# Where the transfers of weight sums are queued, and which engine spreads the probabilities

## The chip, the cores and the metric

The kernel runs on one core of a Trainium2 chip. The metric is device time in microseconds from one launch to its end; lower is better. The core has a matrix engine (TensorE, PE in the profile, with its weight loads as PEld), VectorE (DVE), ScalarE (ACT), GpSimd (POOL) and SyncE (SP). SP and POOL issue most of the DMA transfers.

## What is computed

One layer of a hybrid decoder trunk on 256 positions of 2048 channels, in float32. The input is normalised and projected at once into the inputs of three branches and their gates:

```
h = RMSNorm_pre(x); p = h @ w_in
A: GLU -> causal depthwise conv (31) -> LayerNorm -> swish -> @ w_a_out
B: gelu(uv); u * (tril(W_s) LN(v) + b) per 128-position chunk -> @ w_b_out
C: sparse attention: shared queries, separate K/V for compressed / selected / window -> @ w_c_out
y = (g_A*A + g_B*B + g_C*C) @ w_o ;  x = x + RMSNorm_post(y)
h = RMSNorm_pre(x); u = causal_dwconv3(h @ w_up); x = x + RMSNorm_post((silu(u_g) * u_v) @ w_down)
```

The compressed keys and values of branch C come from blocks of 32 positions: `hid = silu(blocks @ w1)`, then `hid @ w2`. The probabilities over the compressed blocks multiply the compressed values, and the other two branches of the attention are added.

## The kernel before, in words

**Products.** Each float32 weight tile of 128x1024 is fetched by SP into one of five buffers (`fetch`, L117), rounded by ScalarE into a high part (L199) and subtracted by VectorE into a low part (L200). TensorE multiplies high by high, high by low and low by high; the two parts of the activations stay in SBUF. Four buffers of each part lie between the splits and TensorE. In the later stages the same is done at L1011 and the products at L1055.

**Products saved.** For part of the gate columns, the output projection and the down projection, four blocks of a product over pairs of 128x512 weight blocks are made with seven products instead of eight (`Seven`). These need sums and differences of weight blocks. The sums are made long before by DMA alone: `ahead_steps` lists, for each quadruple of blocks, a copy into a buffer in DRAM, a second copy where three or four sums are wanted, and transfers that add onto what has been copied. `ahead_by(mark, n)` has POOL wait until a marked value is there (the copy into `tick`, L159, shown at the line of the helper, L129) and then issue the next `n` transfers of the list. `pooled` holds all of these in one order on POOL; a transfer that adds waits on POOL for the copy it adds to. There are 204 transfers in the list: 64 for the gates, 16 for the output projection, 124 for the down projection.

**Order of the stages.** First the second half of branch B's input, then branch A's input (16 transfers behind it, two for each of eight steps), the first half of branch B's input (16 more), the compression's input, the keys, the values, the queries (16, two for each of eight steps, L796). Then `branch`: for four quarters of 512 columns, merge gates and the outputs of branch B (4, 8, 8 and 8 transfers behind a quarter, L1204). Then `outs_a`, the second branch's outputs in the title of the change: the outputs of branch A in four quarters (8 behind each, L1226). Then the merge gates by `Seven` (`gates_7`), the outputs of branch C, the output projection, the up projection, the down projection. What is left of the list is spread over 42 of the 44 steps of the up projection (L1638).

**Background work.** Work that isn't a plain product lies in a queue of generators, `bg`: branch B's normalisation, branch A's convolution and normalisation, the compression (`cmp_prep`, `cmp_gen`), the attention (`attn`). `pump(ns)` is called between plain products and runs generators until the sum of the nanoseconds that they yield reaches the budget (6500 a call in `branch` and `outs_a`); what is yielded is a booking, not a wait. Once the attention has begun (the mark "attn"), the budget of a call is multiplied by `RUSH`, 0.85. The order on each engine follows from this order of emission and a scheduler's estimate of when each instruction could start; at run time each engine keeps that order.

**Compression.** `cmp_prep` has POOL clear the last column of a buffer (L687), then VectorE and ScalarE form the two parts of the blocks (`bk`). `cmp_gen` fetches `w1` in four pieces and multiplies into `zp` (L709, L711), booking 2300 ns for each piece. It starts once the second quarter of the merge gates is at its third part (the mark "outputs").

**Attention.** Eight units (two halves of the positions, two groups of heads, selected and window) each make scores, weights and values. For every second unit, four in all, the transposed probabilities over the compressed blocks are spread over four heads by one multiplication of 128x512 elements (L990), on POOL, into `spread`, a part of the buffer `vbd`. TensorE reads it at L922 as the first product into the unit's output `O`.

Of the kernel before, what the change touches and what calls it, by code (L numbers as in the profile page):

```python
# [45 lines left out]

GP, GREST = [0, 1, 2, 3], list(range(8, KT))
OP, OREST = [0, 1, 2, 4], [6, 7, *range(10, KT)]
BA, BB, BC, BG, RUSH, SUMS_AT = 2100, 2200, 2200, 6500, 0.85, 4
PR = 1000  # L50
NW0, _ = 34, 6
S1, S2, S3 = 6, 12, 14
# [12 lines left out]
def block(ctx: ExitStack, tc: tile.TileContext, x, xf, x0, fp, cst, rows, sgw, w1, w2, wf_a, wt_bv, wf_bu, wf_c,  # L65
# [604 lines left out]
    spread = vbd[:, 2:6]  # L670
# [30 lines left out]
    def cmp_gen(kv):  # L701
        bk = bk_box[kv]
        zp = bank([128, 2, 256], f"zp{kv}")
        for q in range(4):
            hi, lo = piece(w1[kv, :, q * 1024:q * 1024 + 1024], 1024)
            for i in range(4):
                jj = 4 * q + i
                st = bk[:, jj].rearrange("p a n -> p (a n)")
                PE.matmul(zp[:, 0], lhsT=st, rhs=hi[:, i * 256:i * 256 + 256], start=(jj == 0), stop=(jj == 15),  # L709
                          skip_group_check=True)  # L710
                PE.matmul(zp[:, 1], lhsT=st, rhs=lo[:, i * 256:i * 256 + 256], start=False, stop=(jj == 15),  # L711
                          skip_group_check=True)
            yield 2300
        zs = [q1(f"zs{kv}{a}") for a in range(2)]
        for a in range(2):
            S.activation(zs[a], zp[:, a], AF.Copy)
        hp = bank([128, 2, 64], f"hp{kv}")
        for h in range(2):
            for a in range(2):
                PE.matmul(hp[:, h], lhsT=zs[a][:, h * 128:h * 128 + 128], rhs=sel, start=(a == 0), stop=(a == 1))  # L720
        w2s = q1(f"w2s{kv}", (128, 2, 128))
        nc.sync.dma_start(w2s, w2[:, kv])
        hid = P1.tile([128, 2, 64], F32, tag="hid", bufs=2, name=f"hid{kv}")
        th = q1(f"hth{kv}", (128, 2, 64))
        S.activation(th, hp, AF.Tanh, scale=0.5)
        hidden.append(V.scalar_tensor_tensor(hid, th, 1.0, hp, op0=ALU.add, op1=ALU.mult).ins)
        yield 400
        if kv == 0:
            ps = bank([128, 64], "kcp")
            for h in range(2):  # L730
                PE.matmul(ps, lhsT=w2s[:, h], rhs=hid[:, h],
                          start=(h == 0), stop=(h == 1))
            V.tensor_mul(kcb.rearrange("p g n -> p (g n)"), ps, cs[:, K_KM:K_KM + 64])
            yield 200
        else:
            hr = [q1(f"hidr{h}", (128, 2, 128)) for h in range(2)]
            for h in range(2):
                for gg in range(2):
                    V.tensor_copy(hr[h][:, gg].rearrange("p (j m) -> p j m", j=4),
                                  hid[:, h, gg * 32:gg * 32 + 32][:, None, :].to_broadcast([128, 4, 32]))  # L740
            yield 800
            for gg in range(2):
                ps = bank([128, 128], f"vcp{gg}")
                for h in range(2):
                    PE.matmul(ps, lhsT=hr[h][:, gg], rhs=w2s[:, h], start=(h == 0), stop=(h == 1))
                V.tensor_mul(vbd[:, gg], ps, cs[:, K_BM:K_BM + 128])
                yield 270
# [17 lines left out]
    for i in range(4):  # L765
        pc = ftile(wf_c[4 + i], hT)
        fsum(pc, kk[:, i % 2, i // 2], rb=rb)
        pump(BUDGET)
    vsw = kkv[:, 1].rearrange("p (t c) -> p t c", t=2)
    gsg = P1.tile([128, 2, 48], F32, name="gsg")  # L770
# [22 lines left out]
    for i in range(8):  # L793
        pq = ftile(wf_q[i], hT)
        fsum(pq, qf[:, i], scale=0.125, rb=rb)
        ahead_by(qf[:, i, 0:1], 2)  # L796
        pump(BUDGET)


# [43 lines left out]
    pct = {}  # L843
# [133 lines left out]
    def attn():  # L977

        units = [Unit(qt, gg, br) for qt in (1, 0) for gg in range(2) for br in range(2)]
        yield from in_turn(lnz_gen(), apart(cmp_attn(1)), apart(units[0].scores()))  # L980
        marks.add("A")
        Ct_box["t"] = s16(P1, [128, 8, 2, T], R, "Ct")
        for n, u in enumerate(units):
            if n + 1 < len(units):
                if n == 1:
                    yield from in_turn(apart(cmp_attn(0)), units[n + 1].scores())
                else:
                    yield from units[n + 1].scores()
            if u.at[2] == 0:
                G.tensor_mul(spread, pct[u.at[0]][:, u.at[1]][:, None, :].to_broadcast([128, 4, 128]),  # L990
                             cs[:, K_RJ:K_RJ + 4][:, :, None].to_broadcast([128, 4, 128]))
            yield from u.weights()
            if SUMS_AT <= n < SUMS_AT + 4:
                yield from input_sums(n - SUMS_AT)
            if u.at[2] == 0:
                O = bank([128, 4, 128], "O" + u.nm)
            yield from u.values(O)
# [149 lines left out]
    def branch():  # L1147

        for cb in range(4):
            pg = [PS.tile([128, 512], F32, tag="acc", name=f"pg0{cb}{t}") for t in range(2)]  # L1150
            for q in range(4):
                hs = granule(wt_g[cb * 4 + q])
                for k in range(4 * q, 4 * q + 4):
                    hi, lo = hs[(k % 4) // 2]
                    c = slice((k % 2) * 512, (k % 2) * 512 + 512)
                    for t in range(2):
                        ts = slice(t * 128, t * 128 + 128)
                        with ExitStack() as order:
                            if (cb, k) == (1, 0):
                                order.enter_context(tc.issue_after(norm["v"]))  # L1160
                            mm_t(pg[t], hT[:, k, 0, ts], hT[:, k, 1, ts], hi[:, c], lo[:, c], k == 0, k == KT - 1)
                if (cb, q) == (0, 2):
                    until("m")
                    debt[0] = 0.0
                elif q < 3:
                    if (cb, q) == (1, 2):
                        marks.add("outputs")
                    pump(BUDGET)
            tgs = {}
            for t in range(2):  # L1170
                for a in range(2):
                    tgs[t, a] = q1(f"mg0{cb}{t}{a}")
                    with tc.high_priority(offset=int(PR)):
                        gated[0] = S.activation(tgs[t, a], pg[t][:, a * 256:a * 256 + 256], AF.Tanh,
                                                scale=rh[:, t:t + 1]).ins
            marks.add("gates")
            pump(BUDGET)
            py = [PS.tile([128, 512], F32, tag="acc", name=f"py0{cb}{t}") for t in range(2)]
            for q in range(2):
                hs = granule(wt_p[cb * 2 + q])  # L1180
                if cb == 0 and q == 0:
                    until("B")
                act = Bt_box["t"]
                for k in range(4 * q, 4 * q + 4):
                    hi, lo = hs[(k % 4) // 2]
                    c = slice((k % 2) * 512, (k % 2) * 512 + 512)
                    for t in range(2):
                        ts = slice(t * 128, t * 128 + 128)
                        with ExitStack() as order:
                            if (cb, k) == (0, 7):  # L1190
                                until("v")
                                debt[0] = max(debt[0], 0.0)
                                order.enter_context(tc.issue_after(norm["v"]))
                            pe_last[0] = mm_t(py[t], act[:, k, 0, ts], act[:, k, 1, ts], hi[:, c], lo[:, c], k == 0, k == 7)
                if q == 0:
                    pump(BUDGET)
            for t in range(2):
                for a in range(2):
                    cc = slice(cb * 512 + a * 256, cb * 512 + a * 256 + 256)
                    y = mac[:, t, cc]  # L1200
                    with tc.high_priority(offset=int(PR)):
                        V.scalar_tensor_tensor(y, tgs[t, a], 1.0, py[t][:, a * 256:a * 256 + 256], op0=ALU.add,
                                               op1=ALU.mult)
            ahead_by(mac[:, 0, cb * 512:cb * 512 + 1], (4, 8, 8, 8)[cb])  # L1204
            pump(BUDGET)

    def outs_a():

        for cb in range(4):
# [13 lines left out]
            for t in range(2):  # L1223
                with tc.high_priority(offset=int(PR)):
                    V.tensor_copy(ya[:, t, cb * 512:cb * 512 + 512], py[t])
            ahead_by(ya[:, 0, cb * 512:cb * 512 + 1], (8, 8, 8, 8)[cb])  # L1226
            pump(BUDGET)

    def m_sums(n):
# [511 lines left out]
    i = 0  # L1741
# [260 lines left out]
```

## Time and profile before

| | us |
|---|---|
| three timed runs | 1578.43, 1580.05, 1580.97 |
| their median | 1580.05 |
| the profiled execution | 1574.79 |
| its span, first to last instruction | 1573.1 |
| mean granted clock of TensorE | 0.995 |

The profiled execution is one run of the program, recorded instruction by instruction. Busy times are for each engine; the waits of an engine name the instruction that ended the wait; the chain of waits follows the last instruction back to what released it; a granted clock of 0.50 means that TensorE ran at half speed in that stretch.

### The profile page before, as it was taken

The page shows a single profiled execution, that of the slowest core. Times are in us where ns is not written, and L with a number is a line of the kernel's source. Part 1 is how long each engine was busy: PE and PEld are TensorE (multiplying, and loading weights), DVE is VectorE, ACT ScalarE, POOL GpSimd, SP SyncE. Part 2 cuts the span into 40 slices and gives each one's busy share as a digit, 9 for nine tenths or more (in the row PEclk, how much of TensorE's full clock was granted, in tenths as well). Part 3 has the DMA queues.
Part 4 walks back from the last instruction along what each step waited for, and adds up shares of the span by engine and source line. Part 5 has one row for each costly group of instructions (what it writes and reads, how often), then busy time and mean ns, then how long its engine had stood idle before and what let it go on. Part 6 is the DMA issues. An engine that isn't in the chain of part 4 may idle for free.

```text
span 1573.1 us, 23354 instructions
## 1 busy us (share of the span) xinstructions
PE 1555.0 (99%) x8101; PEld 1317.6 (84%) x8101; DVE 1320.8 (84%) x2229; ACT 969.3 (62%) x1536; POOL 219.7 (14%) x351
## 2 busy tenths in 40 slices
PE   9999999999999898999999999999999999999998
PEld 8888889888777576888888888888888888888887
DVE  7899999787675477977986898888888887899898
ACT  7645454456767665656665766565656665677774
POOL 1011340211112220000000022222121212100000
PEclk9999999999999999999999999999999999999999
DMA  9687997998779997767774699999999999989895
GB/s 369 198 267 235 284 274 217 297 276 280 202 211 274 256 292 260 257 235 250 269 250 175 219 290 321 309 293 288 273 273 274 265 270 290 310 286 349 311 372 217
DMA packets 130712, 426.13 MB, mean 271 GB/s; under 512 B 15009, under 2 KB 16785, under 8 KB 129825
## 3 DMA queue, kind: packets, MB, share of 16 engines
q1 hardware_dynamic: 99648, 329.46, 59.7%
q0 software_dynamic: 30368, 94.52, 25.5%
q8 instruction: 63, 1.03, 0.3%
q10 hardware_dynamic: 576, 0.66, 0.1%
q14 instruction: 57, 0.46, 0.1%
HBM read 416.45 MB, written 90.44 MB: 322 GB/s over the span
## 4 chain that ended last, share of the span: by engine, by line
PE 90%; DMA 6%; DVE 2%; issue 1%; ACT 1%; POOL 1%; SPq 0%; DVEq 0%; ACTq 0%; POOLq 0%
PE ps L228 29%; PE ps L235 15%; PE pg L1055 7%; PE pd1a L1055 4%; PE pd0b L1055 4%; PE pd0a L1055 3%; PE pd1b L1055 3%; DMA ahead<-in_wt_dq_dram 2%; DMA ahead<-in_wt_oq_dram 2%; PE poa L1055 2%; PE py L250 2%; PE py L251 2%; PE py L249 2%; PE pg L250 1%; PE pg L251 1%; PE pg L249 1%
## 5 line engine op out<-in xcount | busy, mean ns | idle before, releaser
L200 DVE TENSOR_TENSOR wlo<-wraw,whi 128x1024 fp32r<-128x1024 f32 (+1 forms) x344 | 417.5, 1218 | 91.7 <-ACT whi L199 73.3
L199 ACT ACTIVATE whi<-wraw 128x1024 fp32r<-128x1024 f32 (+1 forms) x344 | 361.7, 1056 | 206.3 <-PE ps L228 117.2
L228 PE MATMUL ps<-h2T,whi 128*128 128x512 f32 x1360 | 317.2, 390 | 0.0
L228 PEld LDWEIGHTS ps<-h2T,whi 128*128 128x128 f32 x1360 | 252.4, 188 | 50.4
L235 PEld LDWEIGHTS ps<-h2T,wlo 128*128 128x128 f32 x1360 | 169.4, 192 | 3.6
L235 PE MATMUL ps<-h2T,wlo 128*128 128x256 f32 x1360 | 170.7, 283 | 0.0
L228 PE MATMUL ps<-hT,whi 128*128 128x512 f32 x640 | 151.9, 390 | 0.0
L228 PEld LDWEIGHTS ps<-hT,whi 128*128 128x128 f32 x640 | 117.9, 188 | 23.0
L1011 DVE TENSOR_TENSOR wlowraw<-wraw,whiwraw 128x1024 fp32r<-128x1024 f32 x74 | 89.8, 1222 | 42.8 <-ACT whiwraw L1011 40.8
L1011 ACT ACTIVATE whiwraw<-wraw 128x1024 fp32r<-128x1024 f32 x74 | 78.0, 1059 | 55.2 <-PE pg L1055 13.2
L556 DVE SCALAR_TENSOR_TENSOR cv<-hb,fps,cv 128x256 f32<-128x256 f32 x240 | 104.6, 478 | 0.1
L1055 PE MATMUL pg<-whiwraw,hT 128*128 128x512 f32 x256 | 85.3, 407 | 1.2 <-ACT whiwraw L1011 1.2
L1613 ACT ACTIVATE fa<-fs,fps 128x256 f32<-128x256 f32 x88 | 52.7, 599 | 53.5 <-DVE fs L274 51.7
L235 PEld LDWEIGHTS ps<-hT,wlo 128*128 128x128 f32 x640 | 81.1, 191 | 2.5
L235 PE MATMUL ps<-hT,wlo 128*128 128x256 f32 x640 | 82.8, 283 | 0.0
L129 POOL DMA_DIRECT2D ahead<-in_wt_dq_dram x91 | 69.4, 895 | 74.7 <-DMA ahead<-in_wt_dq_dram 72.1
L271 ACT ACTIVATE t<-ps 128x256 f32<-128x256 f32 x125 | 47.5, 381 | 49.5 <-PE ps L235 27.0
L129 POOL DMA_DIRECT2D ahead<-ahead x53 | 43.8, 827 | 206.9 <-DMA ahead<-in_wt_dq_dram 74.7
L129 POOL COPY tick<-gh 128x1 f32<-128x1 f32 x44 | 34.3, 781 | 236.1 <-ACT gh L1621 236.1
L1055 PEld LDWEIGHTS pg<-whiwraw,hT 128*128 128x128 f32 x256 | 49.6, 194 | 14.4 <-issue 2.1
L1614 DVE SCALAR_TENSOR_TENSOR fa<-fs,fps,fa 128x255 f32<-128x255 f32 x88 | 42.3, 481 | 16.6 <-ACT fa L1613 16.5
L1055 PE MATMUL pg<-wlowraw,hT 128*128 128x512 f32 x128 | 51.8, 404 | 3.3 <-DVE wlowraw L1011 3.3
(2519 smaller groups left out, 3313.7 us busy)
## 6 DMA issues: line engine op xcount, KB each, us to landing
wraw<-in_wf_up_dram SPq DMA_DIRECT2D x176, 512.0 KB, 6.4
ahead<-in_wt_dq_dram POOLq DMA_DIRECT2D x74, 512.0 KB, 9.4
wraw<-in_wt_p_dram SPq DMA_DIRECT2D x48, 512.0 KB, 5.9
wraw<-in_wt_dq_dram SPq DMA_DIRECT2D x33, 512.0 KB, 5.6
wraw<-in_wf_a_dram SPq DMA_DIRECT2D x32, 512.0 KB, 5.0
ahead<-in_wt_gq_dram POOLq DMA_DIRECT2D x32, 512.0 KB, 9.6
wraw<-in_wt_g_dram SPq DMA_DIRECT2D x32, 512.0 KB, 6.4
wraw<-in_wt_gp_dram SPq DMA_DIRECT2D x32, 512.0 KB, 5.4
```

The costliest lines, as they stand in the source:

```text
L129: in_pool[:] = [op(*args, **kw).ins]
L199: S.activation(hi[:, :n], raw[:, :n], AF.Copy)
L200: V.tensor_sub(lo[:, :n], raw[:, :n], hi[:, :n].bitcast(F32))
L228: ins = PE.matmul(ps, lhsT=ws[k // 8][0][:, c:c + 128], rhs=mov[:, k], start=bool(k == 0 and first), stop=bool(k == n - 1 and not first), ...
L235: ins = PE.matmul(ps[:, 1], lhsT=ws[k // 8][1][:, c:c + 128], rhs=mov[:, k, 0], start=bool(k == 0 and not first), stop=bool(k == n - 1 and ...
L249: PE.matmul(ps, lhsT=xh, rhs=hi, start=first, stop=False)
L250: PE.matmul(ps, lhsT=xh, rhs=lo, start=False, stop=False)
L271: S.activation(t1, ps[:, 1], AF.Copy)
L556: V.scalar_tensor_tensor(ca[:, j], hb[:, j, k:k + T], w(j, k), ca[:, j], op0=ALU.mult, op1=ALU.add)
L1011: seq[eng] = [op(*args, **kw).ins]
L1055: ins = PE.matmul(bank, lhsT=a[x], rhs=w[y], start=first and j == 0, stop=bool(last and j == 2), skip_group_check=more).ins
L1613: S.activation(a, s, AF.Identity, bias=fps[:, C_FB + f:C_FB + f + 1], scale=w[2])
```

## The change

The list of transfers and its order stay as they are; what changes is behind which step they are issued. One goes behind each of the four key projections (four in all), 20 instead of 16 behind the queries (two and three in turn), 8 instead of 4 behind the first quarter of `branch`, and 12 instead of 32 behind `outs_a` (8 and 4, none behind its last two quarters). Before the up projection 100 transfers are issued instead of 108, and the up projection gets the other 104. The multiplication that spreads the probabilities goes from POOL to VectorE. A piece of the compression is booked at 3200 instead of 2300 ns. `RUSH` goes from 0.85 to 1.0, so that a call of `pump` runs as much background work during the attention as before it.

```diff
-BA, BB, BC, BG, RUSH, SUMS_AT = 2100, 2200, 2200, 6500, 0.85, 4
+BA, BB, BC, BG, RUSH, SUMS_AT = 2100, 2200, 2200, 6500, 1.0, 4
...
                 PE.matmul(zp[:, 1], lhsT=st, rhs=lo[:, i * 256:i * 256 + 256], start=False, stop=(jj == 15),
                           skip_group_check=True)
-            yield 2300
+            yield 3200
...
         pc = ftile(wf_c[4 + i], hT)
         fsum(pc, kk[:, i % 2, i // 2], rb=rb)
+        ahead_by(kk[:, i % 2, i // 2, 0:1], 1)
         pump(BUDGET)
...
         fsum(pq, qf[:, i], scale=0.125, rb=rb)
-        ahead_by(qf[:, i, 0:1], 2)
+        ahead_by(qf[:, i, 0:1], 2 + i % 2)
         pump(BUDGET)
...
             if u.at[2] == 0:
-                G.tensor_mul(spread, pct[u.at[0]][:, u.at[1]][:, None, :].to_broadcast([128, 4, 128]),
+                V.tensor_mul(spread, pct[u.at[0]][:, u.at[1]][:, None, :].to_broadcast([128, 4, 128]),
                              cs[:, K_RJ:K_RJ + 4][:, :, None].to_broadcast([128, 4, 128]))
...
-            ahead_by(mac[:, 0, cb * 512:cb * 512 + 1], (4, 8, 8, 8)[cb])
+            ahead_by(mac[:, 0, cb * 512:cb * 512 + 1], (8, 8, 8, 8)[cb])
             pump(BUDGET)
...
                     V.tensor_copy(ya[:, t, cb * 512:cb * 512 + 512], py[t])
-            ahead_by(ya[:, 0, cb * 512:cb * 512 + 1], (8, 8, 8, 8)[cb])
+            if cb < 2:
+                ahead_by(ya[:, 0, cb * 512:cb * 512 + 1], (8, 4)[cb])
             pump(BUDGET)
```

## The prediction

> **What bounds the kernel now.** I read the head of the page first, then the waits of PE, then the granted clock in short windows around them.
>
> ```profile
> span 1573.1 us, 23354 instructions
> ## 1 busy us (share of the span) xinstructions
> PE 1555.0 (99%) x8101; PEld 1317.6 (84%) x8101; DVE 1320.8 (84%) x2229; ACT 969.3 (62%) x1536; POOL 219.7 (14%) x351
> ```
>
> PE is the bound: 1573.1 - 1555.0 = 18.1 us of the span is not PE's. The change takes no matmul away and adds none, so it can only win what PE waits for, and what a wait costs PE afterwards. The waits of PE (engine, line, what for; total, times, longest):
>
> ```profile
> PE O L922 <- POOL vbd L990: 6.2, 1, 6.2
> PE pg L1055 <- DVE wlowraw L1011: 3.3, 2, 2.5
> PE pg L1055 <- ACT whiwraw L1011: 1.2, 1, 1.2
> PE warm L343 <- DVE wz L340: 1.1, 1, 1.1
> PE py L250 <- DVE wlo L200: 0.8, 1, 0.8
> PE py L249 <- ACT whi L199: 0.5, 1, 0.5
> ```
>
> Three places matter. One wait of 6.2 us is for the spread probabilities (the buffer vbd, line 990), which POOL writes. Three waits, 3.3 + 1.2 = 4.5 us, are for split weights at the start of the second pair of merge-gate columns. Two, 0.8 + 0.5 = 1.3 us, are in the stage of the second branch, where the compression runs. The rest lies at the two ends of the kernel, which the change doesn't touch. The windows of 5 us (length, then busy PE, PEld, DVE, ACT, POOL; then the granted clock, DMA share, GB/s) show what follows a wait:
>
> ```profile
> 540.00:545.00 5.00, 0.80 (x4) 0.33 (x3) 0.54 (x3) 2.32 (x10) 1.88 (x3) 0.96 1.02 388
> 545.00:550.00 5.00, 2.99 (x5) 1.76 (x6) 0.00 (x0) 0.00 (x0) 1.96 (x3) 0.50 1.05 227
> 550.00:555.00 5.00, 5.00 (x20) 4.00 (x20) 2.45 (x2) 3.70 (x8) 1.37 (x2) 0.85 0.59 201
> ...
> 605.00:610.00 5.00, 2.50 (x7) 1.87 (x7) 5.00 (x8) 2.45 (x3) 0.00 (x0) 0.61 0.25 68
> 610.00:615.00 5.00, 5.00 (x18) 3.97 (x17) 3.50 (x4) 1.30 (x2) 0.00 (x0) 0.71 0.78 240
> ```
>
> The clock is halved for (0.04 + 0.50 + 0.15) x 5 / 0.5 = 6.9 us around the first wait, and for (0.39 + 0.29) x 5 / 0.5 = 6.8 us around the second group. PE's share of those stretches costs half its length. Now the chain of waits (start, length, what), which names what was late:
>
> ```profile
> 351.80 5.38 DMA wraw<-in_wt_p_dram
> ...
> 547.01 2.07 PE O L922 x2
> ...
> 584.85 13.19 DMA wraw<-in_wt_gp_dram
> ```
>
> and POOL's timeline, which says why:
>
> ```profile
> 285.50 0.82 POOL L129 DMA_DIRECT2D ahead<-ahead  x1 [5.42 <-DMA ahead<-in_wt_gq_dram]
> ...
> 315.57 1.35 POOL L129 DMA_DIRECT2D ahead<-in_wt_gq_dram  x2 [1.76 <-DMA ahead<-in_wt_gq_dram]
> 334.91 0.19 POOL L129 COPY tick<-mac 128x1 f32<-128x1 f32 x1 [18.00 <-DVE mac L1202]
> ...
> 337.64 0.86 POOL L687 MEMSET bt<- 128x16 f32 x4
> ...
> 545.59 1.37 POOL L990 TENSOR_TENSOR vbd<-pct,cs 128x512 f32<-128x512 f32 x1
> ...
> 585.57 1.90 POOL L129 DMA_DIRECT2D ahead<-in_wt_dq_dram  x3 [1.76 <-DMA ahead<-in_wt_dq_dram]
> ```
>
> POOL issues the transfers of weight sums in a fixed order, and each sum waits on POOL for the copy it adds to. Where they queue up, ten transfers take 315.57 - 285.50 = 30.1 us: 3.0 us each. The 32 behind the second branch's outputs (line 1226, which this text calls the outputs' 32) are issued until 585.57; the fourth spread sits among them and starts at 545.59, when PE has waited since 547.0 - 6.2 = 540.8. The load of gate weights that lands after 13.19 us runs beside the last of them.
>
> **The change part by part.** The sum is made against the profiled execution, 1574.79 us (span 1573.1). The three timed runs have a median of 1580.05, 5.26 us more; I carry that over unchanged.
>
> *Spread by VectorE, and 20 of the 32 moved.* Either edit alone would free PE from the 6.2 us. Of the clock's halved 6.9 us, from 544.6 to 551.5, PE waited until 547.0, so 4.5 us of matmuls ran at half speed: 2.2 us. Together **-8.4**. Four multiplications go to VectorE. The nearest row there is the subtraction of the same size:
>
> ```profile
> L932 DVE TENSOR_TENSOR Ct<-O,Ct x4: 682/688/691, 477.1 to 568.0; 128x512 fp32r<-128x512 f32 x4
> ```
>
> Four times 0.69 = 2.8 us, between nothing and 2.8; I take nothing, because VectorE idles in that stage (0.54 of 5 us busy from 540 to 545). They now wait in VectorE's queue for the transposed probabilities and for PE's last read of the buffer, with weight splits behind them; the third rival prices that.
>
> *What moves out from behind the outputs* is 20 transfers: at 3.0 us each POOL is done about 60 us before 585.57 + 1.9, near 527, before the gate stage loads its weights. Then the load that landed after 13.19 us should land like the 5.38 us of the chain's other row, and the second group of waits goes: 4.5 us, plus the halved clock from 606.1 to 612.9, where PE stood until 607.65 and then ran 5.2 us at half speed: 2.6. Together **-7.1**. The Trainium skill ("TensorE: Matmul & The Clock Gate", Part 1) gives about 3.4 us of idling as what halves the clock. No single wait of the second group is that long, so by the page, an estimate, these waits would cost 4.5 alone and the forecast would be 2.6 us higher; the windows show a halved clock, and the sum goes by them.
>
> *Where they go.* Four go behind the key projections, just ahead of the queries, where the second row below has its slice at 0.7 of the DMA engines (slice 7 of 40, 236 to 275 us): nothing. Four go to the queries and four to the first quarter of the second branch, where DMA is at 0.9 or more (slices 8 and 9). Eight go to the 42 steps of the up projection, 104 instead of 96 there, beside DMA shares of 0.9 all along:
>
> ```profile
> PEclk9999999999999999999999999999999999999999
> DMA  9687997998779997767774699999999999989895
> ```
>
> ```profile
> SPq L117 <- DVE wlo L200: 443.3, 214, 8.2
> ```
>
> The loads of weights mostly wait for a free buffer (214 times, 443 us), not the reverse; that lead hides the eight, so nothing. If the lead were gone, each late load would cost what the second place costs now.
>
> *Queries and first quarter.* The queries now have 20 transfers. Four are issued before 285.50, and then 16 remain: 16 x 3.0 = 48, until 333.5, just before the copy at 334.91 that opens the eight of the first quarter. The first of these waits for the last sum to land. POOL's four memsets for the compression, now at 337.64, stand behind at least four transfers and come later. How late they may be:
>
> ```profile
> 344.92 0.42 DVE L698 TENSOR_TENSOR bk<-bt,bk 128x256 fp32r<-128x256 f32 x1
> ```
>
> ```profile
> L709 PEld LDWEIGHTS zp<-whi,bk x32: 187/192/192, 350.9 to 378.5; 128*128 128x128 f32 x32
> ```
>
> The operands are ready at 345.3, PE wants them at 350.9: 5.6 us of slack, so a memset after 343.2 begins to cost. I take **+1.0**, between 0 (behind four, as now) and 18.1 (the fifth rival).
>
> *Compression less dense.* Each of its eight pieces is booked at 3200 ns instead of 2300, so 7.2 us more of budget; at 6500 a call the first call still runs three pieces, the later ones shift. It could take away the 1.3 us there, and the extra transfers could lengthen them: between -1.3 and +10.2 (second rival). I take 0, nearest to the small wait that is there.
>
> *Attention denser.* A call now gives 6500 instead of 5525 ns of background work, 18% more. The two windows where ScalarE is full (ACT is the fourth busy column):
>
> ```profile
> 410.00:420.00 10.00, 10.00 (x44) 6.82 (x44) 7.58 (x31) 10.00 (x30) 0.00 (x0) 1.00 0.29 100
> 420.00:430.00 10.00, 10.00 (x46) 8.29 (x45) 6.06 (x14) 10.00 (x30) 2.95 (x5) 1.00 0.71 154
> ```
>
> ```profile
> L199 ACT ACTIVATE whi<-wraw 128x1024 fp32r<-128x1024 f32 (+1 forms) x344 | 361.7, 1056 | 206.3 <-PE ps L228 117.2
> L228 PE MATMUL ps<-h2T,whi 128*128 128x512 f32 x1360 | 317.2, 390 | 0.0
> ```
>
> A split of 1.06 us serves twelve matmuls of 317.2 / 1360 = 0.23 us, 2.8 us, so weights take 7.6 of the 20 us; the attention's 12.4 would grow by 18%, 2.2 us too much, while PE waits for nothing there now. Between 0 and 2.2; I take **+1.0**, since four buffers of splits lie ahead of PE.
>
> The sum: -8.4 - 7.1 + 1.0 + 0 + 1.0 = -13.5. Profiled 1561.3, median **1566.5** us.
>
> **The rivals.**
> 1. *The second group of waits stays*, because the gate stage's own loads fill the DMA engines: +7.1, 1573.6. For it: 13.19 us is far from 5.38. Against it: three transfers were issued at 585.57, right beside that load.
> 2. *The contention only moves.* The weights for the compression and the second branch land after 13.19 instead of 5.38 us: +7.8, and +2.4 for a halved clock (the mean of 2.2 and 2.6): +10.2, 1576.7. For it: the chain at 351.80 runs through exactly such a load. Against: POOL issues one at a time per 3.0 us, and PE waited for nothing beside that rate in slice 8. The Trainium skill ("DMA: Bandwidth & Descriptors", Issuing engines are not separate DMA queues) says that all queues share 16 engines and interleave; no run shown here moves a transfer, so the trace can't yet say.
> 3. *The change doesn't do what it says:* PE waits for VectorE's spread instead, 8.4 us given back: 1574.9. Against: VectorE idled while PE waited.
> 4. *Both one and three:* +15.5, 1582.0, no change that can be told.
> 5. *Slower: the memsets stand behind all eight transfers.* They start at 334.91 + 8 x 3.0 = 358.9 instead of 337.64, 21.3 us later; less the slack, PE waits 15.7 us for the compression, plus 2.4 of halved clock: 18.1 in place of my 1.0, so +3.6 in all, 1583.7. It decides from a start after 343.2, and turns the sum's sign at 355 (343.2 + 14.5 - 2.4). For it: the memsets come after the copy at 334.91 in POOL's order today. Against: today they come right behind four transfers, and the fifth must wait for a sum.
>
> **How the numbers follow.** A measurement of this kernel can tell about 0.2%, 3.2 us, from no change. Forecast 0.44 (its own range 1562 to 1572, from the terms' bounds near it), rivals 0.12, 0.12, 0.08, 0.09 and 0.15. Faster: 0.44 + 0.12 + 0.08 and half of the second rival, which lies at the edge, 0.06: 0.70. Same: the other 0.06 and 0.07 of the fourth: 0.13. Slower: 0.15 + 0.02: 0.17. The range 1562 to 1582 leaves out the fifth rival and little else. Its lower end is near all the waits gone: 8.4 + 7.1 + 1.3 = 16.8, 1563.2.
>
> **What would show it.** Right: PE's waits have no spread of 6 us; the clock's windows have no halved stretch from 540 to 615; POOL's last transfer behind the outputs is issued near 527; the gate weights after it land in 5 to 6 us. The memset's start against 343 decides between my +1.0 and the fifth rival; ACT's full stretch after 410 shows the attention's term. Wrong: a new wait of PE for zp's operands, for splits of wt_p or w near 350, or for vbd from VectorE, each with a halved clock behind it.

## The result and the profile after

| | before, us | after, us |
|---|---|---|
| median of four timed runs | 1580.07 | 1562.74 |
| lowest to highest | 1578.43 to 1580.97 | 1559.78 to 1563.63 |
| the profiled execution | 1574.79 | 1563.63 |
| its span | 1573.1 | 1561.9 |

The ratio is 0.9888, with a 95% interval from 0.9871 to 0.9905: 1.1% faster, and the median is 3.8 us under the forecast of 1566.5. The profiled executions stand 11.2 us apart, the medians 17.3; the first experiment below bears on that difference.

The waits of PE after the change (engine, line, what for; total, times, longest). Lines behind 768 have moved by one or two:

```profile
PE hp L720 <- ACT zs L716: 1.3, 1, 1.3
PE py L249 <- ACT whi L199: 1.3, 2, 0.7
PE warm L343 <- DVE wz L340: 1.1, 1, 1.1
PE pg0s L1056 <- DVE Ct L933: 1.1, 1, 1.1
PE py L250 <- DVE wlo L200: 0.6, 1, 0.6
PE pg L250 <- DVE wlo L200: 0.5, 1, 0.5
```

Neither the 6.2 us for the spread nor the 4.5 us at the gate weights is there. In their place stand 1.3 + 1.3 + 0.6 + 0.5 = 3.7 us in the stage of the compression, where 1.3 us stood before, and 1.1 us at the end of the attention. The windows of 5 us answer to those shown of before (the third number from the right is the granted clock):

```profile
540.00:545.00 5.00, 5.00 (x31) 3.63 (x31) 0.63 (x4) 5.00 (x20) 0.00 (x0) 1.00 0.68 179
545.00:550.00 5.00, 5.00 (x28) 3.21 (x25) 4.72 (x20) 4.65 (x11) 0.00 (x0) 1.00 0.41 113
550.00:555.00 5.00, 5.00 (x26) 3.79 (x25) 2.27 (x5) 5.00 (x20) 0.00 (x0) 1.00 0.82 308
605.00:610.00 5.00, 5.00 (x24) 4.12 (x23) 4.92 (x6) 3.93 (x5) 0.00 (x0) 1.00 0.82 277
610.00:615.00 5.00, 5.00 (x24) 4.12 (x23) 4.92 (x6) 3.93 (x5) 0.00 (x0) 1.00 0.93 306
```

PE is busy throughout at full clock. A new stretch of halved clock lies elsewhere:

```profile
390.00:395.00 5.00, 3.65 (x20) 2.90 (x19) 2.36 (x2) 2.19 (x4) 2.17 (x4) 1.00 1.01 383
395.00:400.00 5.00, 5.00 (x16) 3.93 (x15) 4.39 (x9) 4.08 (x7) 0.53 (x2) 0.66 1.07 322
```

That is 0.34 x 5 / 0.5 = 3.4 us at half speed, all of it with PE at work: 1.7 us lost. The chain of waits names the loads that were late there (start, length, what). The wait of `hp` for `zs` belongs to them too: in this chain, ScalarE splits the second of these loads first, at 392.1, and only then makes `zs`.

```profile
352.94 9.74 DMA wraw<-in_wt_p_dram
...
380.87 11.16 DMA wraw<-in_wt_g_dram
```

And POOL's timeline shows the queue that the change made:

```profile
335.06 0.18 POOL L129 COPY tick<-mac 128x1 f32<-128x1 f32 x1 [4.67 <-DVE mac L1203]
339.13 0.82 POOL L129 DMA_DIRECT2D ahead<-ahead  x1 [3.89 <-DMA ahead<-in_wt_gq_dram]
339.68 0.80 POOL L129 DMA_DIRECT2D ahead<-in_wt_gq_dram  x1
341.39 1.34 POOL L129 DMA_DIRECT2D ahead<-in_wt_gq_dram  x2 [0.91 <-DMA ahead<-in_wt_gq_dram]
342.46 0.56 POOL L687 MEMSET bt<- 128x16 f32 x4
350.38 0.81 POOL L129 DMA_DIRECT2D ahead<-ahead  x1 [7.37 <-issue]
...
535.41 0.83 POOL L129 DMA_DIRECT2D ahead<-in_wt_dq_dram  x1 [0.71 <-DMA ahead<-in_wt_dq_dram]
```

The memsets come behind four of the eight transfers, at 342.5; the last transfer behind the outputs is issued at 535.4, not at 585.6. The loads of gate weights behind it, in the view of DMA issues for the stretch from 580 to 620 (count, KB each, median us to landing), land like this:

```profile
wraw<-in_wt_gp_dram SPq DMA_DIRECT2D x8, 512.0 KB, 5.1
```

The same view of before, from 580 to 600 (up to 620 it has one load more, and a median of 12.5):

```profile
wraw<-in_wt_gp_dram SPq DMA_DIRECT2D x4, 512.0 KB, 12.7
```

### The profile page after: what moved, and what is told of

Same layout as the page of the kernel before. It is cut to its first block, busy times and chain, and to the rows that moved or that the text cites. A ratio compares the mean times of both kernels' runs of the same rounds, so it can differ in the third digit from the quotient of the medians.

```text
span 1561.9 us, 23350 instructions
## 1 busy us (share of the span) xinstructions
PE 1551.4 (99%) x8101; PEld 1315.6 (84%) x8101; DVE 1322.3 (85%) x2233; ACT 970.2 (62%) x1536; POOL 220.9 (14%) x349
## 4 chain that ended last, share of the span: by engine, by line
PE 97%; DMA 1%; DVE 1%; ACT 1%; issue 0%; DVEq 0%; ACTq 0%
PE ps L228 29%; PE ps L235 15%; PE pg L1056 8%; PE pd1a L1056 4%; PE pd0b L1056 4%; PE pd0a L1056 3%; PE pd1b L1056 3%; PE py L250 3%; PE py L251 3%; PE py L249 3%; PE poa L1056 2%; PE pg L251 1%; PE pg L250 1%; PE pg L249 1%; PE s L854 1%; PE po L249 1%
## 5 line engine op out<-in xcount | busy, mean ns | idle before, releaser
L129 POOL COPY tick<-gh 128x1 f32<-128x1 f32 x44 | 37.5, 853 | 186.3 <-ACT gh L1623 186.3
L272 DVE TENSOR_TENSOR t<-ps,t 128x256 f32<-128x256 f32 x125 | 52.4, 420 | 0.5 <-ACT t L271 0.5
```

Source lines behind the costliest of these rows:

```text
L129: in_pool[:] = [op(*args, **kw).ins]
```

## The experiments

My theory was that both stalls come from the 32 transfers behind the outputs, one through POOL's queue and one through traffic beside the gate weights, and that what the change pays is traffic in the compression's stage. The rivals were that the spread's engine makes the gain, and that the order of the background work (the two bookings) does. Waits in the table are PE's, in us, from one profiled execution each; medians and ratios come from the timed runs, each against runs of the kernel before in the same set. There are four sets (the change itself; r1 to r4; r5 to r8; r9 to r12), whose medians of the kernel before are 1580.07, 1577.51, 1578.15 and 1575.91 us, so a difference of a few us between medians of two sets isn't certain, and the kernel after was timed in the first set alone.

| kernel | median, us | ratio to before (95%) | compression, 345 to 400 | spread | gate weights | end of attention |
|---|---|---|---|---|---|---|
| before | | | 1.3 | 6.2 | 4.5 | 0 |
| r1_again: before | 1574.42 | 0.9991 (0.9975 to 1.0007) | 1.3 | 2.8 | 4.4 | 0 |
| r2_spread | 1565.39 | 0.9928 (0.9909 to 0.9947) | 1.1 | 0 | 5.0 | 0 |
| r3_moved | 1568.01 | 0.9939 (0.9918 to 0.9961) | 7.1 | 0 | 0 | 0 |
| r4_dense | 1575.56 | 0.9988 (0.9974 to 1.0001) | 0.9 | 11.4 | 3.5 | 1.1 |
| r5_moved_spread | 1565.37 | 0.9920 (0.9904 to 0.9936) | 8.2 | 0 | 0 | 0 |
| after | 1562.74 | 0.9888 (0.9871 to 0.9905) | 3.7 | 0 | 0 | 1.1 |
| r6_after_2300 | 1568.30 | 0.9938 (0.9914 to 0.9962) | 5.3 | 0 | 0 | 1.5 |
| r7_after_rush85 | 1571.48 | 0.9958 (0.9941 to 0.9975) | 2.4 | 0 | 0 | 6.0 |
| r8_after_q2c4 | 1556.79 | 0.9863 (0.9847 to 0.9878) | 0 | 0 | 0 | 1.1 |
| r9_q2c4_old_bookings | 1558.10 | 0.9879 (0.9860 to 0.9898) | 1.1 | 0 | 0 | 0 |
| r10_q2c4_pool_spread | 1557.69 | 0.9874 (0.9855 to 0.9893) | 0 | 0 | 0 | 1.1 |
| r11_after_c4 | 1557.94 | 0.9880 (0.9860 to 0.9899) | 0.5 | 0 | 0 | 1.1 |
| r12_q2c4_rush115 | 1561.54 | 0.9896 (0.9876 to 0.9916) | 0.8 | 0 | 0 | 3.0, in its middle |

**r1_again: the kernel before, unchanged.**

> The kernel before, unchanged, profiled a second time. Its first profiled execution took 1574.79 us, 5.3 us less than the median of its timed runs. Theory of varying waits: the two stalls of PE (for the spread probabilities 6.2 us, at the gate weights 4.5 us) hang on when transfers land, so a second profile shows other lengths, together 2 to 6 us longer, and the span follows them. Rival, a constant overhead in timed runs: the waits are again 6.2 and 4.5 us within 0.5 and the span is 1573.

The profiled execution took 1572.10 us. Its waits of PE, the first two lines:

```profile
PE O L922 <- POOL vbd L990: 2.8, 1, 2.8
PE pg L1055 <- DVE wlowraw L1011: 2.5, 1, 2.5
```

The wait for the spread is 2.8 us instead of 6.2, in the same kernel, and no halved clock follows it; 3.4 us of it follow the waits at the gate weights instead of 6.8, and 3.4 stand in the compression's stage. So the waits do vary, though these are shorter, not longer as I expected. 24 timed runs of the kernel before, beside these first experiments, lie between 1572.21 and 1583.42 us; their mean granted clock falls from 0.996 in the fastest to 0.992 in the slowest, and 0.004 of 1575 us are 6.3 us, the most that the lower clock can account for. The most likely reading is that the stalls hang on when transfers land, and the time of the kernel with them: the 11.2 us between the profiled executions and the 17.3 between the medians are then the same change, seen from different runs of a scattered time. The waits of the unprofiled runs aren't on record.

**r2_spread, r3_moved, r4_dense: each part alone, on the kernel before.**

```diff
-                G.tensor_mul(spread, ...
+                V.tensor_mul(spread, ...
```

> The kernel before with the spread on VectorE alone; all 32 transfers stay behind the second branch's outputs. My theory (each stall has its own cause): the 6.2 us wait goes, the waits at the gate weights stay at 4.5 us or grow with the transfers that still run beside them; 6 to 10 us faster than before, ratio 0.994 to 0.996. Rival (the spread is the whole gain): ratio 0.989, no wait left at the gate weights. Rival (VectorE takes over the wait): PE waits for vbd from VectorE, ratio 0.999 to 1.002.

The wait for the spread goes, the gate weights still cost 3.2 + 1.0 + 0.8 us, and the whole is 0.9928: a little faster than the 0.994 I expected, which the interval still holds, but not the 0.989 of a spread that is the whole gain. The second stall needs the other part.

r3_moved makes all four changes of `ahead_by` in the change's diff and nothing else.

> The kernel before with the 20 transfers moved and nothing else; the spread stays on POOL, the bookings stay. My theory (POOL's queue and the traffic beside the gate weights are the cause of both stalls): POOL issues the last transfer behind the outputs near 535, the fourth spread runs without PE waiting more than 1 us, the gate weights land in time, the compression's stage pays about what it pays after the change (3.7 us of waits, a stretch of halved clock); ratio 0.988 to 0.992. Rival (the spread on VectorE is needed): the wait for vbd stays at 3 us or more, ratio 0.994 or above.

With the spread still on POOL, PE waits for neither the spread nor the gate weights: the last transfer behind the outputs is issued at 539.3, and the fourth spread starts right behind it at 539.8. So the first stall has two remedies. The ratio, 0.9939, is above what I expected all the same, for the compression's stage pays more than after the change. The largest row of PE's waits in that kernel, and a row of its chain of waits:

```profile
PE py L249 <- ACT whi L199: 5.7, 2, 5.1
```

```profile
354.06 11.49 DMA wraw<-in_wt_p_dram
```

PE stood 5.1 us for a load of the second branch's weights that took 11.5 us to land; before the change the load at this place took 5.4.

r4_dense has the two bookings:

```diff
-BA, BB, BC, BG, RUSH, SUMS_AT = 2100, 2200, 2200, 6500, 0.85, 4
+BA, BB, BC, BG, RUSH, SUMS_AT = 2100, 2200, 2200, 6500, 1.0, 4
...
-            yield 2300
+            yield 3200
```

> The kernel before with the two bookings alone: 3200 ns for a piece of the compression, no reduction of the attention's budget. My theory: both stalls stay, within 2 us, and the 1.3 us of waits in the compression's stage may go: ratio 0.998 to 1.002. Rival (the order of the background work makes the gain): ratio 0.996 or less, with the spread's wait under 3 us, because the attention is through before the transfers queue up. Rival on the other side (ScalarE becomes the bound): new waits of PE for ScalarE between 400 and 540 of 2 us or more, ratio above 1.002.

The bookings alone change nothing that can be told: 0.9988, with 1 inside the interval. That both stalls stay within 2 us was wrong: the wait for the spread is 11.4 us in this profile, since the fourth spread stands behind six transfers of its group instead of four, and it starts at 557.6.

**r5_moved_spread: both remedies, old bookings.**

> The kernel before with the 20 transfers moved and the spread on VectorE, without the two bookings. My theory (moving alone frees both stalls; the spread's engine adds nothing then): the same waits as with the transfers moved alone, near 7 us in the compression's stage and none for vbd, ratio 0.992 to 0.996. Rival (the bookings add nothing): as fast as the whole change, 0.989 within 0.002.

0.9920: at the edge of what my theory expected. Once the transfers are gone, the engine of the spread adds little: the interval overlaps that of r3_moved. The compression's waits, 8.2 us, are the highest of all.

**r6_after_2300 and r7_after_rush85: the change with one booking taken back.**

> The kernel after with a piece of the compression booked at 2300 ns again. My theory (with eight more transfers beside them, the loads of the second branch land late, and a denser compression makes PE wait longer for them): waits of PE between 345 and 400 of 6 us or more against 3.7 after the change, 2 to 5 us slower than the kernel after, ratio to before 0.990 to 0.993. Rival (the booking is neutral): waits within 1 us of the kernel after, ratio 0.989.

5.3 us of waits in the compression's stage against 3.7, less than the 6 I had set, and 0.9938, a little above what I had set. As far as one profile of each can tell, the wider booking of the compression softens what the transfers cost there.

> The kernel after with the attention's budget reduced to 0.85 again. My theory (the denser attention wins nothing, PE is the bound): the wait of 1.1 us of the gate products for the attention's last output goes, other waits stay, ratio 0.988 within 0.002. Rival (a denser attention keeps PE from waiting later): new waits of 2 us or more after 540, ratio 0.990 or more.

This expectation was wrong: the rival, new waits behind 540, is what came. Two of them:

```profile
PE pp L915 <- ACT ep L901: 2.8, 1, 2.8
PE O L854 <- ACT ep L920: 1.6, 1, 1.6
```

They end at 564 and 560, with 3.4 us of halved clock behind them. At its end PE has to wait for the attention. Why is not settled: the attention's first scores start at 401.8 here, earlier than in the kernel after (404.8) and in r5_moved_spread (406.3), which has the same 0.85 and no such wait. What the runs do show is that the two bookings belong together: 3200 without 1.0 (0.9958) costs more than both of the old ones (r5_moved_spread, 0.9920), with intervals that don't meet.

**r8_after_q2c4: the eight transfers taken back from the compression's stage.**

```diff
-        ahead_by(qf[:, i, 0:1], 2 + i % 2)
+        ahead_by(qf[:, i, 0:1], 2)
...
-            ahead_by(mac[:, 0, cb * 512:cb * 512 + 1], (8, 8, 8, 8)[cb])
+            ahead_by(mac[:, 0, cb * 512:cb * 512 + 1], (4, 8, 8, 8)[cb])
```

> The kernel after with the eight transfers taken back from the queries and the first quarter of the second branch; they go to the up projection, which then has 112. My theory (contention in the compression's stage is what the change pays): waits of PE between 345 and 400 fall from 3.7 us to 1.5 or less, no halved clock there, 2 to 5 us faster than the kernel after, ratio to before 0.985 to 0.988; the up projection shows no wait. Rival (the late loads come from the order of the background work, not from the transfers): waits there of 3 us or more, ratio 0.989 or more. Rival (the up projection has no room): new waits of PE after 900.

All the waits of PE that are left in this kernel:

```profile
PE warm L343 <- DVE wz L340: 1.1, 1, 1.1
PE pg0s L1056 <- DVE Ct L933: 1.1, 1, 1.1
```

Nothing is left in the compression's stage, no clock is halved before the last microseconds, and the up projection carries its 112 transfers without a wait. It is the fastest kernel of the study: 1556.28 to 1557.16 us, below every run of the kernel after (1559.78 and more, in another set of runs). By the ratios the intervals of the two overlap (0.9847 to 0.9878 against 0.9871 to 0.9905), so that it is faster rests on these absolute times and on the waits that are gone. Its four runs also lie within 0.9 us, where 24 runs of the kernel before spread over 11. Few waits and little scatter go together in r9 and r10 too (1.1 and 1.0 us), but not everywhere: the 12 runs of r4_dense, with both stalls, lie within 3.4 us.

**r9 to r12, on r8 or beside it.** r9 is r8 with 2300 and 0.85.

> The version with the eight transfers taken back (r8) with both bookings as before the change, 2300 and 0.85. Theory (the bookings only soften what the eight transfers cost): without those transfers the bookings win little; the 1.3 us of waits in the compression's stage that the kernel before has come back, the wait of 1.1 us for the attention's last output may go: 0 to 2 us slower than r8, ratio to before 0.986 to 0.988. Rival (the bookings are worth something by themselves): 3 us or more slower than r8.

1558.10, 1.3 us slower than r8 (which ran in another set; the intervals of the ratios overlap), with 1.1 us of waits back in the compression's stage: as expected, the bookings win little by themselves.

r10 is r8 with `G.tensor_mul` for the spread.

> r8 with the spread on POOL again. Theory (with 12 transfers behind the outputs POOL reaches the fourth spread in time, whichever engine has it): as fast as r8 within 2 us, no wait for vbd over 1 us. Rival (POOL is still busy with transfers when the spread is wanted): a wait of PE for vbd from POOL of 2 us or more.

1557.69 and no wait for the spread: the engine makes no difference that can be told once POOL's queue is short.

r11 is the kernel after with `(4, 8, 8, 8)` behind the quarters of `branch`, and 20 behind the queries.

> The kernel after with only the four transfers of the first quarter taken back (they go to the up projection); the queries keep 20. Theory (it is the four of the first quarter that run beside the loads of the second branch): waits between 345 and 400 at 1.5 us or less, within 2 us of r8, ratio 0.986 to 0.988. Rival (the backlog of the queries' 20 carries the contention in): waits of 2 us or more there, ratio 0.988 or more.

0.5 us of waits in the compression's stage in place of 3.7, 1557.94: of the waits that the eight transfers brought, those by the four behind the first quarter are nearly all. The ratio itself, 0.9880, can't be told from the 0.9888 of the kernel after.

r12 is r8 with `RUSH` at 1.15.

> r8 with the attention's budget raised to 1.15. Theory (the last wait, 1.1 us of the gate products for the attention's last output, comes of the attention ending too late): it goes, 1 us faster than r8, not over what the comparison can tell. Rival (ScalarE is full by then): new waits of PE for ScalarE between 400 and 560 of 2 us or more, 2 us or more slower than r8.

The rival was right. The 1.1 us at the end go, but new waits come in the middle of the attention:

```profile
PE O L854 <- ACT ep L920: 1.8, 1, 1.8
...
PE pp L915 <- ACT pt L920: 0.7, 1, 0.7
```

6.8 us of halved clock follow them, and the kernel is 4.8 us slower than r8, and 3.9 slower than r10, which ran in the same set. ScalarE does come to hold PE up, between 1.0 and 1.15: from 470 to 475 it is busy all 5.0 us, and PE 2.7.

## Why the prediction was right, point by point

The terms, against the profiled executions (11.2 us apart):

| term | predicted, us | measured, us |
|---|---|---|
| the wait for the spread, with its halved clock | -8.4 | -8.4 |
| the waits at the gate weights, with theirs | -7.1 | -7.1 |
| memsets behind transfers | +1.0 | 0 |
| compression's stage | 0 | +2.4 of waits, +1.7 of halved clock |
| attention denser | +1.0 | +1.1 |
| sum | -13.5 | -10.3, of 11.2 between the spans |

The 0.9 us that are left aren't assigned to a place.

- **The two large terms were right, and so was their cause.** r2_spread takes away the first and leaves the second; r3_moved takes away both with the spread still on POOL. The last transfer came 8 us later than I had put it (535.4 against 527): the 20 transfers less brought it forward by 51 us, 2.6 each, where I had taken the 3.0 of the queries' stage.
- **Right with the wrong emphasis:** the text says that either edit alone would free PE from the spread's wait. Both do, but since the moved transfers do it anyway, VectorE's part of the gain is nothing that r10 or r5 can tell. VectorE did come to wait for PE's last read of the buffer (6.5 us in two waits), as the third rival had it, and PE did not wait in turn.
- **The memsets** start at 342.5, just ahead of the 343.2 from which they would cost, behind four transfers, not eight. PE doesn't wait for zp. The term was 0, and the fifth rival didn't come.
- **The compression's stage was mis-sized.** The sum took 0 and gave the second rival, contention that moves, 10.2 us and a chance of 0.12. It came in part, at 4.1 us: from 345 to 400 the median time from issue to landing went from 6.6 to 10.9 us for the second branch's weights (in_wt_p) and from 4.9 to 7.9 for the gates' (in_wt_g). r8 and r11 show that the transfers moved there are the cause, the four behind the first quarter above all; in r8 these loads land in 8.3 and 6.7 us, and PE waits for none of them. "Nearest to the small wait that is there" was no reason: from 345 to 400 the DMA engines were busy for 0.89 of the time before, and traffic was added to it (0.96 after).
- **The attention's term had the right size for the wrong reason.** ScalarE had no part in it: PE waits for ScalarE nowhere between 400 and 560 after the change. The 1.1 us is the gate products' wait behind VectorE's last step of the attention. It is there in r4_dense, and it goes at 1.15, where ScalarE's waits come instead. Why it is there at 1.0 and not with the old bookings was not settled; the order of emission changes on all engines.
- **The eight transfers in the up projection** cost nothing, nor do the eight more of r8.
- **The median** fell further than the sum, most likely because the profiled execution of before was one of its faster runs (r1_again), while that of after, 1563.63, was the slowest of its four. I carried the 5.26 us between profile and median over as constant. They weren't: the range's lower end, "all the waits gone", was put at 1563.2, and the median fell below it with 4.8 us of waits left. So that the forecast came within 3.8 us is partly luck: the profiled time was 2.3 us over its 1561.3, and the scatter went the other way.

## What to carry to other kernels

A queue in which transfers wait for each other on the issuing engine is a wait for everything else behind them on that engine; count the transfers behind each step, and price the last of them by the rate at which they go when they pile up (2.6 to 3.0 us each here). When transfers are moved, look where the DMA engines and the loads of that stage have room: the compression's stage, with the DMA engines at 0.89 already, paid back 4 of 15 us, while the up projection, at 0.95, took 16 more without a wait of PE. There SyncE's loads waited for VectorE, whose splits free the buffers, for 378 of the 420 us from 900 to 1320 before the change; from 345 to 400 it was 41 of 55. A time that scatters from run to run can be a sign that PE waits for transfers, but a steady time is no proof that it doesn't (r4_dense).

## What the runs showed of the hardware

The stretches of halved clock have only three lengths in all these profiles, apart from the one at the end of the program: 3.4, 6.8 and 10.2 us, one, two and three times 3.41 (windows of 0.1 us give 3.41, 6.83 and 10.24). Within one execution they also start a whole number of 3.413 us apart: at 544.64 and 606.08 before the change, 18 times, and at 371.86 and 607.38 in r1_again, 69 times. The Trainium skill ("TensorE: Matmul & The Clock Gate", Part 1) speaks of a free-running window of activity of about 3.4 us, and these lengths and starts agree with it. They don't agree with its rule of thumb that a gap must exceed some 3.4 us of idling: after the change a wait of 1.3 us, with four of 0.5 to 0.7 in the 35 us ahead of it, was followed by 3.4 us at half speed, and in r12 waits of 0.7, 1.8 and 0.5 us by 6.8; in r1_again, a wait of 2.8 us was followed by none. Two waits of 0.5 and 0.8 us in the compression's stage were followed by 3.4 us in r1_again and by none in the first profile of the same kernel. The measurement decides: here even short waits can cost a window of half speed, and whether they do differs from run to run. What decides it isn't shown.
